# One square per norm: a 1024-column sum of squares in place of two halves, and an epsilon that GpSimd adds

## The chip, the cores and the metric

The program runs on one core of a Trainium2 chip. The metric is the device time of one execution in microseconds (us). Before the change three runs gave 1055.66, 1057.25 and 1059.41 us; the median is 1057.25.

The engines are called by their names in the profile: PE (TensorE, matrix products), ACT (ScalarE), DVE (VectorE), POOL (GpSimd) and SP (SyncE, which issues the transfers). PEld is PE's loading of weights.

## The reference

Two decoder layers on 256 tokens of 1024 columns. Each layer is three half-layers (six in all): a SwiGLU, a mixer (sparse attention in the first layer, differential attention in the second) and a second SwiGLU. Each half-layer has a norm ahead and a norm behind:

```python
def rmsnorm(x, g):
    xf = x.astype(jnp.float32)
    y = xf * lax.rsqrt(jnp.mean(xf * xf, axis=-1, keepdims=True) + EPS)
    return (y * g.astype(jnp.float32)).astype(x.dtype)
...
h = modulate(rmsnorm(x, pre_norm[i, 0]), sh0, sc0)
y = swiglu(h, ffn_w_gate[i, 0], ffn_w_up[i, 0], ffn_w_down[i, 0])
x = x + FFN_HALF * g0[:, None, :] * rmsnorm(y, post_norm[i, 0])
```

The shifts, scales and gates come from a product of a conditioning vector with `ada_w`, in 18 pieces of 1024 columns.

## The kernel before

The 256 tokens are two tiles of 128, `t` = 0 and 1, called t0 and t1 here. The residual stream is in `X[t]`, 128 rows of 1024 columns; two more columns hold a constant whose scaled square is the epsilon. A product is computed for each tile by itself, with weights as the moving operand: a block of 128 rows of a weight matrix is read by SP into `raw`, rounded by ACT (`whl` at line 234, "CAST") and its rest taken by DVE (line 235), because each product is made of three matmuls of rounded parts and rests. So a block of weights is six matmuls for a tile (three kinds, two halves of the columns). There are seven buffers for such blocks (`WBUFS = 7`), and each block is used by t0 and then by t1 before its buffer is free. t1 runs five to seven blocks behind t0 (`LAG`, `LAGX`).

Where one half-layer ends and the next begins, a tile goes through a chain. Its last matmul of `y` (`ydown`, `ydsa` or `ydiff`) ends; `postnorm` takes the sum of squares of `y` on ACT, raises it to the power −0.5 on POOL, and adds to `X[t]` on DVE: first `u`, `y` times the gate, then `x`, `u` times the power plus the old `x`. Then `prenorm` takes the sum of squares of the new `X[t]` on ACT (`normed`), the power on POOL, and DVE makes `h` in two steps (`modulated`): `x` times `g` (line 414), times the power plus `sh` (line 415). PE transposes `h` into `ps_x` (line 418), eight times 128x128, ACT and DVE split that into `HT`, and the next product begins. There are five such places between the six half-layers, and the end of the program is a sixth with `postnorm` alone.

`u` reads `y` in PSUM after ACT's square of it: the framework lets the two engines read that tile in turn. A scheduler sets the order of the instructions on each engine ahead of time, by a model of their durations and by priorities (`urgent()` raises that of the norms); on the chip each engine then keeps to that order. Between the instructions of the chain it places other work, above all casts and subtractions of weights (lines 234 and 235) and the accumulations of `ada_w` on DVE (line 311, `pg`, `g` or `sh`). POOL also clears the buffers of these accumulations (line 302).

The lines that the change touches are `normed` (lines 397 to 408) and `postnorm` (from line 458).

Of the kernel before, what the change touches and what calls it, by code (L numbers as in the profile page):

```python
# [8 lines left out]
F32 = mybir.dt.float32  # L9
F32R = mybir.dt.float32r  # L10
I32 = mybir.dt.int32
AF = mybir.ActivationFunctionType
OP = mybir.AluOpType
# [5 lines left out]
EPS = 1e-6  # L19
# [30 lines left out]
def trunk(ctx, tc, x, c, positions, ada_w, ada_b, pre_norm, post_norm, ffn_w_gate, ffn_w_up,  # L50
          ffn_w_down, dsa_w_in, dsa_w_out, diff_w_in, diff_w_out, diff_lambda, diff_subln, out):
    nc = tc.nc
# [5 lines left out]
    small = ctx.enter_context(tc.tile_pool(name="small", bufs=2))  # L58
# [5 lines left out]
    def tmp(name, shape=(128, 1024), dt=F32):  # L64
        return tmpp.tile(list(shape), dt, name=name, tag="tmp")
# [13 lines left out]
    def half(hf):  # L79
        return slice(hf * 512, (hf + 1) * 512)  # L80

    def flat(t):
        return t.rearrange("p a b -> p (a b)")
# [6 lines left out]
    for t in range(2):  # L90
        xt = consts.tile([128, D + 2], F32, name=f"x{t}")
        nc.vector.memset(xt[:, D:D + 2], EPS_COL)
        X.append(xt)
    epsc = consts.tile([128, 1], F32, name="epsc")
# [302 lines left out]
    def normed(t):  # L397

        xt = X[t]
        ss = small.tile([128, 2], F32, name="ss", tag="ss", bufs=4)  # L400
        r = small.tile([128, 1], F32, name="rstd", tag="rstd1", bufs=4)
        for hf, w in enumerate((512, 513)):
            junk = tmp("junk", (128, 513))
            nc.scalar.activation(junk[:, 0:w], xt[:, hf * 512:hf * 512 + w], AF.Square, scale=1.0 / 32,
                                 accum_out=ss[:, hf:hf + 1])
        nc.scalar.activation(r, ss[:, 0:1], AF.Identity, bias=ss[:, 1:2])
        nc.gpsimd.tensor_tensor(r, r, mhalf[:, 0:1], op=OP.pow)  # L407
        return r, HT[:, t]

# [13 lines left out]
    def first_h(t, k):  # L423

        for q, (f0, n) in enumerate(PIECES):
            if f0 == k * 128 and q not in FIRST:
                FIRST[q] = True
                first_part(q)
                if q == 0:
                    FIRST["x"] = []  # L430
                    for u in range(2):
                        nc.sync.dma_start(X[u][:, 0:D], x[0, u * 128:(u + 1) * 128, :])
                        FIRST["x"].append(normed(u))
                for u in range(2):
                    modulated(0, u, *FIRST["x"][u], k, n // 128)
        return FIRST["x"][t][1]

    def prenorm(t, n):
        r, hT = normed(t)
        for q in range(2):  # L440
            modulated(n, t, r, hT, 4 * q, 4)
        return hT
# [13 lines left out]
                                           op0=OP.mult, op1=OP.subtract)  # L456

    def postnorm(t, y, n, last=False):
        ss = small.tile([128, 2], F32, name="ssy", tag="ssy", bufs=4)
        r = small.tile([128, 1], F32, name="rstdy", tag="rstd1", bufs=4)  # L460
        u = tmp("u")
        for hf in range(2):
            junk = tmp("junk", (128, 513))
            nc.scalar.activation(junk[:, 0:512], y[:, hf, :], AF.Square, scale=1.0 / 32, accum_out=ss[:, hf:hf + 1])
            if hf == 0:
                nc.scalar.activation(ss[:, 0:1], ss[:, 0:1], AF.Identity, bias=epsc)
        nc.scalar.activation(r, ss[:, 0:1], AF.Identity, bias=ss[:, 1:2])  # L467
        nc.gpsimd.tensor_tensor(r, r, mhalf[:, 0:1], op=OP.pow)  # L468
        for hf in range(2):
            nc.vector.tensor_tensor(u[:, half(hf)], y[:, hf, :], MOD[n]["pg"][:, half(hf)], op=OP.mult)  # L470
        for hf in range(2):
            h = half(hf)
            nc.vector.scalar_tensor_tensor(X[t][:, h], u[:, h], r, X[t][:, h], op0=OP.mult, op1=OP.add)
            if last:
                nc.sync.dma_start(out[0, t * 128:(t + 1) * 128, h], X[t][:, h])
# [9 lines left out]
    def ffn(t, n):  # L485
# [86 lines left out]
        with urgent():  # L572
            postnorm(t, y, n, last=(n == 5))
# [50 lines left out]
    def dsa(t, n):  # L624
# [151 lines left out]
        with urgent():  # L776
            postnorm(t, y, n)

    def diff(t, n):
# [134 lines left out]
        with urgent():  # L914
            postnorm(t, y, n)
# [73 lines left out]
```

## Time and profile before

| | |
|---|---|
| median of three runs | 1057.25 us |
| the profiled execution | 1058.01 us |
| its span, first to last instruction | 1056.2 us |
| PE busy | 1015.5 us, 96% |
| DVE busy | 788.6 us, 75% |
| ACT busy | 523.8 us, 50% |
| POOL busy | 45.0 us, 4% |
| mean granted clock of PE | 0.993 |

In a timeline a row gives the start in us, the duration in us, the engine, the line of the kernel, the operation and what it writes and reads; the brackets hold the idle time ahead of it and what ended that. In a row of waits come the engine and what it waited for, then the total in us, the number of times and the longest. In a row of windows the stretch is followed by its length, the busy time of PE, PEld, DVE, ACT and POOL with their instructions, the granted clock of PE, the busy share of the transfer engines and GB/s. In a group there are the total busy us and the mean ns of one.

### The profile page before, as it was taken

The numbers are of one execution on the slowest core, as the hardware profiler recorded it, in microseconds if no ns is written. First come the engines' busy times: TensorE is split into PE (matmuls) and PEld (weight loads), VectorE is DVE, ScalarE is ACT, GpSimd is POOL, SyncE is SP. The second block draws the span as 40 slices with busy tenths as digits, with TensorE's granted clock in tenths as the row PEclk, the third lists the DMA queues.
The fourth block names the chain that finished last, engine by engine and source line by source line (L and its number), as shares of the span: only waits on it lengthen the run. The fifth ranks groups of instructions, "written<-read, shape, count | busy, mean of one in ns | idle before, by whom it ended". The sixth has DMA issues, their size and how long they took to land.

```text
span 1056.2 us, 15311 instructions
## 1 busy us (share of the span) xinstructions
PE 1015.5 (96%) x5936; PEld 873.6 (83%) x5936; DVE 788.6 (75%) x1121; ACT 523.8 (50%) x834; POOL 45.0 (4%) x49
## 2 busy tenths in 40 slices
PE   5999999989999999999999999999999899999997
PEld 2689997769778789998878999887777678999875
DVE  5769887989976977877688967767988575765643
ACT  3354534455575654543455544346477555544432
POOL 1000000001000200000030000001000120000000
PEclk9999999999999999999999999999999999999999
DMA  9959899986443477988757979956653443778431
GB/s 315 343 147 322 313 321 378 347 293 218 148 142 128 155 273 247 352 286 291 271 193 260 314 257 316 316 208 236 260 200 118 153 134 115 243 235 261 183 117 40
DMA packets 93732, 249.48 MB, mean 236 GB/s; under 512 B 6084, under 2 KB 24652, under 8 KB 93660
## 3 DMA queue, kind: packets, MB, share of 16 engines
q1 hardware_dynamic: 93660, 248.52, 68.1%
q8 instruction: 46, 0.75, 0.3%
q14 instruction: 26, 0.21, 0.1%
HBM read 247.44 MB, written 1.05 MB: 235 GB/s over the span
## 4 chain that ended last, share of the span: by engine, by line
PE 57%; issue 20%; DVE 4%; ACT 3%; POOL 2%; DMA 1%; POOLq 0%; DVEq 0%; ACTq 0%
PE ydown L267 15%; PE up L282 9%; PE gate L282 8%; PE gate L267 3%; PE up L267 3%; PE projQd L267 2%; PE projQ L267 2%; PE projV L267 2%; PE projA L267 2%; PE projK L267 2%; PE ydsa L267 1%; POOL rstd L407 1%; DVE whl L235 1%; PE dsaO L752 1%; PE ydiff L267 1%
## 5 line engine op out<-in xcount | busy, mean ns | idle before, releaser
L235 DVE TENSOR_TENSOR whl<-raw,whl 128x1024 fp32r<-128x1024 f32 (+3 forms) x216 | 245.7, 1150 | 98.5 <-ACT whl L234 97.7
L234 ACT CAST whl<-raw 128x1024 fp32r<-128x1024 f32 (+3 forms) x216 | 211.8, 995 | 190.1 <-PE ydown L267 89.5
L282 PE MATMUL gate<-HT,wj 128*128 128x256 f32 x1344 | 166.2, 284 | 1.5 <-DVE wj L212 1.4
L212 DVE TENSOR_TENSOR wj<-raw,wj 128x1024 fp32r<-128x1024 f32 x112 | 134.7, 1221 | 43.1 <-ACT wj L211 42.8
L211 ACT CAST wj<-raw 128x1024 fp32r<-128x1024 f32 x112 | 116.4, 1050 | 100.3 <-DMA raw<-in_ffn_w_up_dram 21.5
L282 PEld LDWEIGHTS gate<-HT,wj 128*128 128x128 f32 x1344 | 163.4, 192 | 2.2 <-DVE wj L212 1.9
L282 PE MATMUL up<-HT,wj 128*128 128x256 f32 x1344 | 164.4, 283 | 0.0
L282 PEld LDWEIGHTS up<-HT,wj 128*128 128x128 f32 x1344 | 162.8, 192 | 0.4
L267 PE MATMUL ydown<-whl,ffj 128*128 128x512 f32 x672 | 157.0, 390 | 2.2 <-DVE whl L235 2.2
L267 PEld LDWEIGHTS ydown<-whl,ffj 128*128 128x128 f32 x672 | 125.7, 188 | 30.6 <-DVE whl L235 3.1
L267 PE MATMUL gate<-whl,HT 128*128 128x480 f32 x384 | 94.3, 392 | 0.4 <-ACT HT L393 0.2
L267 PE MATMUL ydown<-whl,ffa 128*128 128x512 f32 (+1 forms) x368 | 89.3, 393 | 1.9 <-ACT whl L234 1.9
L267 PEld LDWEIGHTS gate<-whl,HT 128*128 128x128 f32 x384 | 72.2, 191 | 16.6 <-ACT HT L393 2.7
L267 PEld LDWEIGHTS ydown<-whl,ffa 128*128 128x128 f32 (+1 forms) x368 | 67.9, 188 | 19.7 <-issue 3.6
L311 DVE SCALAR_TENSOR_TENSOR pg<-araw,scond,pg 128x1024 f32<-128x1024 f32 x48 | 61.4, 1280 | 6.4 <-DMA araw<-in_ada_w_dram 5.8
L267 PE MATMUL up<-whl,HT 128*128 128x480 f32 x288 | 66.0, 381 | 0.0
L267 PEld LDWEIGHTS up<-whl,HT 128*128 128x128 f32 x288 | 53.5, 188 | 8.4 <-ACT sg L512 0.5
L311 DVE SCALAR_TENSOR_TENSOR g<-araw,scond,g 128x1024 f32<-128x1024 f32 x40 | 51.2, 1281 | 7.8 <-DMA araw<-in_ada_w_dram 7.4
L311 DVE SCALAR_TENSOR_TENSOR sh<-araw,scond,sh 128x1024 f32<-128x1024 f32 x40 | 51.2, 1280 | 1.3 <-DMA araw<-in_ada_w_dram 0.8
L468 POOL TENSOR_TENSOR rstdy<-rstdy,mhalf 128x1 f32<-128x1 f32 x12 | 10.2, 850 | 824.2 <-ACT rstdy L467 824.2
L267 PE MATMUL projV<-whl,HT 128*128 128x512 f32 x96 | 28.4, 416 | 0.0
L267 PE MATMUL projQ<-whl,HT 128*128 128x512 f32 x96 | 27.6, 415 | 0.0
(224 smaller groups left out, 1090.7 us busy)
## 6 DMA issues: line engine op xcount, KB each, us to landing
araw<-in_ada_w_dram SPq DMA_DIRECT2D x64, 1024.0 KB
raw<-in_ffn_w_down_dram SPq DMA_DIRECT2D x40, 1024.0 KB
raw<-in_ffn_w_gate_dram SPq DMA_DIRECT2D x56, 512.0 KB
raw<-in_ffn_w_up_dram SPq DMA_DIRECT2D x56, 512.0 KB
raw<-in_ffn_w_gate_dram SPq DMA_DIRECT2D x16, 960.0 KB
raw<-in_diff_w_in_dram SPq DMA_DIRECT2D x12, 1024.0 KB
raw<-in_ffn_w_up_dram SPq DMA_DIRECT2D x12, 960.0 KB
fraw<-in_ada_w_dram SPq DMA_DIRECT2D x32, 256.0 KB
```

Of the source, the lines that this page charges most:

```text
L211: nc.scalar.copy(hl[0], raw)
L212: nc.vector.tensor_tensor(hl[1], raw, hl[0].bitcast(F32), op=OP.subtract)
L234: nc.scalar.copy(hl[:, 0, 0:n], raw[:, j, 0:n])
L235: nc.vector.tensor_tensor(hl[0:r, 1, 0:n], raw[0:r, j, 0:n], hl[0:r, 0, 0:n].bitcast(F32), op=OP.subtract)
L267: nc.tensor.matmul(acc[:, hf, 0:n], lhs, rhs, start=(first and hf not in seen), stop=(last and i % 3 == 2))
L282: nc.tensor.matmul(a[:, b, :], w[:, wp, j, b * 128:(b + 1) * 128], HT[:, :, hp, k0 + j, :], start=(first and j == 0 and i == 0 and b % 2 = ...
L311: nc.vector.scalar_tensor_tensor(a, raw[:, j, :], scond[:, 2 * i + j:2 * i + j + 1], a, op0=OP.mult, op1=OP.add)
L407: nc.gpsimd.tensor_tensor(r, r, mhalf[:, 0:1], op=OP.pow)
L468: nc.gpsimd.tensor_tensor(r, r, mhalf[:, 0:1], op=OP.pow)
L752: nc.tensor.matmul(flat(O)[:, h * 64:(h + 1) * 64], ptb[u][:, i * nb + b, :], v[:, b, :], start=(b == 0), stop=(b == nb - 1), skip_group_c ...
```

## The change

Each sum of squares becomes one ACT operation over all columns, which writes its sum straight to `r`. In the pre-norm it goes over 1025 columns, the constant among them. In the post-norm the epsilon was the bias of an ACT addition and is now added by POOL, ahead of its power.

```diff
     def normed(t):
         xt = X[t]
-        ss = small.tile([128, 2], F32, name="ss", tag="ss", bufs=4)
         r = small.tile([128, 1], F32, name="rstd", tag="rstd1", bufs=4)
-        for hf, w in enumerate((512, 513)):
-            junk = tmp("junk", (128, 513))
-            nc.scalar.activation(junk[:, 0:w], xt[:, hf * 512:hf * 512 + w], AF.Square, scale=1.0 / 32,
-                                 accum_out=ss[:, hf:hf + 1])
-        nc.scalar.activation(r, ss[:, 0:1], AF.Identity, bias=ss[:, 1:2])
+        junk = tmp("junk", (128, 1025))
+        nc.scalar.activation(junk, xt[:, 0:1025], AF.Square, scale=1.0 / 32, accum_out=r)
         nc.gpsimd.tensor_tensor(r, r, mhalf[:, 0:1], op=OP.pow)
         return r, HT[:, t]
...
     def postnorm(t, y, n, last=False):
-        ss = small.tile([128, 2], F32, name="ssy", tag="ssy", bufs=4)
         r = small.tile([128, 1], F32, name="rstdy", tag="rstd1", bufs=4)
         u = tmp("u")
-        for hf in range(2):
-            junk = tmp("junk", (128, 513))
-            nc.scalar.activation(junk[:, 0:512], y[:, hf, :], AF.Square, scale=1.0 / 32, accum_out=ss[:, hf:hf + 1])
-            if hf == 0:
-                nc.scalar.activation(ss[:, 0:1], ss[:, 0:1], AF.Identity, bias=epsc)
-        nc.scalar.activation(r, ss[:, 0:1], AF.Identity, bias=ss[:, 1:2])
+        junk = tmp("junk")
+        nc.scalar.activation(junk, flat(y), AF.Square, scale=1.0 / 32, accum_out=r)
+        nc.gpsimd.tensor_scalar(r, r, EPS, None, op0=OP.add)
         nc.gpsimd.tensor_tensor(r, r, mhalf[:, 0:1], op=OP.pow)
```

The scheduler makes another order of it. The lines of the changed kernel are numbered 4 to 8 lower from here on: 414 became 410, 418 is 414, 464 is 458, 470 is 462, 473 is 465.

PE, at the third place, from the second SwiGLU of the first layer to the first of the second. Before (`ydown` in the first rows is t1's; t0's last `ydown` stands 41 matmuls ahead of the first transposes; `gate` is t0's; the eight `ps_x` at the end are t1's):

```order
L418 MATMUL ps_x<-ident,h 128x128 x4
L267 MATMUL ydown<-whl,ffj 128x512
L418 MATMUL ps_x<-ident,h 128x128 x4
L267 MATMUL gate<-whl,HT 128x480 x38
L418 MATMUL ps_x<-ident,h 128x128 x8
```

With the change (t0's last `ydown` stands 35 matmuls ahead of the first transposes):

```order
L414 MATMUL ps_x<-ident,h 128x128 x4
L267 MATMUL ydown<-whl,ffj 128x512
L414 MATMUL ps_x<-ident,h 128x128 x4
L267 MATMUL gate<-whl,HT 128x480 x4
L267 MATMUL ydown<-whl,ffj 128x512 x2
L267 MATMUL gate<-whl,HT 128x480 x20
L267 MATMUL ydown<-whl,ffj 128x512 x4
L267 MATMUL gate<-whl,HT 128x480 x18
L414 MATMUL ps_x<-ident,h 128x128 x8
```

Six matmuls of t1's `ydown` moved from ahead of t0's transposes to between those of t0's `gate`; t1's last `ydown` now has 18 matmuls between it and t1's transposes. The second, fourth and fifth place have the same pattern, with 31 matmuls ahead of t0's first transposes at each; at the first place PE's order is as before.

ACT, at the fifth place, from the differential attention to the last SwiGLU, t0's chain. Before:

```order
L464 ACTIVATE junk,ssy<-ydiff 128x512 x2
L466 ACTIVATE ssy<-ssy,epsc 128x1
L234 CAST whl<-raw 128x960
L467 ACTIVATE rstdy<-ssy 128x1
L234 CAST whl<-raw 128x960 x2
L404 ACTIVATE junk,ss<-x_79 128x512
L404 ACTIVATE junk,ss<-x_79 128x513
L234 CAST whl<-raw 128x960
L406 ACTIVATE rstd<-ss 128x1
```

With the change:

```order
L458 ACTIVATE junk,rstdy<-ydiff 128x1024
L234 CAST whl<-raw 128x960 x2
L402 ACTIVATE junk,rstd<-x_79 128x1025
L234 CAST whl<-raw 128x960 x3
L393 CAST HT<-ps_x 128x512 x2
```

No cast stands any more between the square and the sum that POOL takes.

DVE, at the same place, t0's chain. Before:

```order
L470 TENSOR_TENSOR u<-ydiff,pg 128x512 x2
L235 TENSOR_TENSOR whl<-raw,whl 128x960
L473 SCALAR_TENSOR_TENSOR x_79<-u,rstdy,x_79 128x512 x2
L235 TENSOR_TENSOR whl<-raw,whl 128x960
L414 TENSOR_TENSOR h<-x_79,g 128x512 x2
L235 TENSOR_TENSOR whl<-raw,whl 128x960
L415 SCALAR_TENSOR_TENSOR h<-h,rstd,sh 128x512 x2
```

With the change:

```order
L462 TENSOR_TENSOR u<-ydiff,pg 128x512 x2
L465 SCALAR_TENSOR_TENSOR x_79<-u,rstdy,x_79 128x512 x2
L235 TENSOR_TENSOR whl<-raw,whl 128x960
L410 TENSOR_TENSOR h<-x_79,g 128x512 x2
L411 SCALAR_TENSOR_TENSOR h<-h,rstd,sh 128x512 x2
```

Two of the three weight subtractions left the chain; the one between `x` and `h` stayed. At the third place an accumulation of line 311 now stands ahead of t0's `u`.

## The prediction

> **What bounds the kernel now.** I read the busy rows of the page first, then the waits of PE, then PE's timeline at the five places where one half-layer ends and the next begins, then ScalarE, VectorE and GpSimd there.
>
> ```profile
> PE 1015.5 (96%) x5936; PEld 873.6 (83%) x5936; DVE 788.6 (75%) x1121; ACT 523.8 (50%) x834; POOL 45.0 (4%) x49
> ...
> PE ps_x L418 <- DVE h L415: 10.7, 9, 3.4
> ```
>
> TensorE works 96% of the span. Nothing that shortens ScalarE (50%) or loads GpSimd (4%) counts by itself; what counts is how long PE stands still. Its largest wait is the transposes `ps_x` of a new half-layer waiting for `h`: 10.7 us. Here are these places, called b1 to b5. Token tile 0 (t0) is transposed first, tile 1 (t1) some 30 matmuls later.
>
> ```profile
> 236.22 1.77 PE L418 MATMUL ps_x<-ident,h 128*128 128x128 f32 x8 [3.39 <-DVE h L415]
> ...
> 347.67 1.38 PE L418 MATMUL ps_x<-ident,h 128*128 128x128 f32 x8 [1.36 <-DVE h L415]
> 349.00 8.76 PE L267 MATMUL gate<-whl,HT 128*128 128x480 f32 x32
> 357.60 1.03 PE L418 MATMUL ps_x<-ident,h 128*128 128x128 f32 x8
> ...
> 523.76 16.03 PE L267 MATMUL ydown<-whl,ffj 128*128 128x512 f32 x70
> 540.64 0.66 PE L418 MATMUL ps_x<-ident,h 128*128 128x128 f32 x4 [0.85 <-DVE h L415]
> 541.97 8.59 PE L267 MATMUL gate<-whl,HT 128*128 128x480 f32 x38
> 550.71 1.29 PE L418 MATMUL ps_x<-ident,h 128*128 128x128 f32 x8 [0.16 <-DVE h L415]
> ...
> 732.03 1.32 PE L418 MATMUL ps_x<-ident,h 128*128 128x128 f32 x8 [0.82 <-DVE h L415]
> 741.00 0.65 PE L418 MATMUL ps_x<-ident,h 128*128 128x128 f32 x4 [0.36 <-DVE h L415]
> 742.33 0.50 PE L267 MATMUL projK<-whl,HT 128*128 128x512 f32 x1 [0.68 <-ACT HT L393]
> ...
> 860.76 0.63 PE L418 MATMUL ps_x<-ident,h 128*128 128x128 f32 x4 [1.02 <-DVE h L415]
> 862.07 8.57 PE L267 MATMUL gate<-whl,HT 128*128 128x480 f32 x38
> 870.74 1.29 PE L418 MATMUL ps_x<-ident,h 128*128 128x128 f32 x8
> ```
>
> The brackets are PE's idle time. t0 costs 3.39, 1.36, 0.85, 0.82 and 1.02 us; t1 costs next to nothing, since 26 to 38 matmuls of t0's next product lie ahead of its transposes. A matmul takes 16.03/70 = 0.229 us with 512 columns and 8.59/38 = 0.226 us with 480. t0's last `y` matmul (E0) ends where its first square starts:
>
> ```profile
> 228.56 0.60 ACT L464 ACTIVATE junk<-ydown 128x512 f32<-128x512 f32 x1 [5.48 <-PE ydown L267]
> 338.63 0.60 ACT L464 ACTIVATE junk<-ydsa 128x512 f32<-128x512 f32 x1 [0.73 <-PE ydsa L267]
> 721.73 0.60 ACT L464 ACTIVATE junk<-ydown 128x512 f32<-128x512 f32 x1 [3.02 <-PE ydown L267]
> 850.55 0.60 ACT L464 ACTIVATE junk<-ydiff 128x512 f32<-128x512 f32 x1 [3.09 <-PE ydiff L267]
> ```
>
> From E0 to t0's transposes at b5 are 860.76 − 850.55 = 10.2 us. What fills them, ScalarE, GpSimd and VectorE in turn (the last four rows are t1's):
>
> ```profile
> 851.89 0.99 ACT L234 CAST whl<-raw 128x960 fp32r<-128x960 f32 x1
> 852.78 0.30 ACT L467 ACTIVATE rstdy<-ssy 128x1 f32<-128x1 f32 x1
> ...
> 853.15 1.46 POOL L468 TENSOR_TENSOR rstdy<-rstdy,mhalf 128x1 f32<-128x1 f32 x1 [9.68 <-ACT rstdy L467]
> 857.99 1.84 POOL L407 TENSOR_TENSOR rstd<-rstd,mhalf 128x1 f32<-128x1 f32 x1 [3.38 <-ACT rstd L406]
> ...
> 851.85 1.29 DVE L470 TENSOR_TENSOR u<-ydiff,pg 128x512 f32<-128x512 f32 x2 [3.13 <-ACT junk L464]
> 853.05 1.15 DVE L235 TENSOR_TENSOR whl<-raw,whl 128x960 fp32r<-128x960 f32 x1
> 854.65 1.42 DVE L473 SCALAR_TENSOR_TENSOR x<-u,rstdy,x 128x512 f32<-128x512 f32 x2 [0.45 <-POOL rstdy L468]
> 855.98 1.15 DVE L235 TENSOR_TENSOR whl<-raw,whl 128x960 fp32r<-128x960 f32 x1
> 857.05 1.29 DVE L414 TENSOR_TENSOR h<-x,g 128x512 f32<-128x512 f32 x2
> 858.26 1.15 DVE L235 TENSOR_TENSOR whl<-raw,whl 128x960 fp32r<-128x960 f32 x1
> ...
> 865.00 0.55 POOL L468 TENSOR_TENSOR rstdy<-rstdy,mhalf 128x1 f32<-128x1 f32 x1 [5.17 <-ACT rstdy L467]
> 868.36 1.45 POOL L407 TENSOR_TENSOR rstd<-rstd,mhalf 128x1 f32<-128x1 f32 x1 [2.80 <-ACT rstd L406]
> ...
> 864.53 1.28 DVE L470 TENSOR_TENSOR u<-ydiff,pg 128x512 f32<-128x512 f32 x2
> 868.12 1.29 DVE L414 TENSOR_TENSOR h<-x,g 128x512 f32<-128x512 f32 x2
> 869.85 1.41 DVE L415 SCALAR_TENSOR_TENSOR h<-h,rstd,sh 128x512 f32<-128x512 f32 x2 [0.44 <-POOL rstd L407]
> ```
>
> Two things are to be seen. A weight cast of 0.99 us stands between the two additions on ScalarE, so the sum reaches GpSimd only at 853.1. And GpSimd's one-column power takes 0.55 us beside `u`, which reads PSUM (865.00), but with a subtraction or product from SBUF on VectorE it ends about 0.4 us after that: 868.36 + 1.45 = 869.81 against 868.12 + 1.29 = 869.41; 853.15 + 1.46 = 854.61 against 853.05 + 1.15 = 854.20.
>
> **The change, part by part.** *Removed from ScalarE:* per norm one square with its accumulator read and one or two additions, 24 norms. ScalarE is idle half the time, so this pays only through the chain. *The single square:* two halves take 851.85 − 850.55 = 1.28 us with the reads; one pass over 1024 columns of PSUM is bounded below by the activation of that shape:
>
> ```profile
> L558 ACT ACTIVATE sgj<-gate 128x1024 f32<-128x1024 f32 x12 | 12.3, 1026 | 20.0 <-PE gate L282 20.0
> ```
>
> I take 1.13 us, 1.03 and the tail of one read (bounds 1.03 and 1.28). It can no longer start on half the columns, which costs nothing behind `y` (both halves follow E0 already). In the pre-norm it waits for both halves of `x`, but the power behind it waits for VectorE's product `h` anyway. *GpSimd's new addition, 12 times:* no such operation is in the trace; the bounds are the power alone (0.55) and at its most held up (1.84). I take 0.55, since it falls beside `u`, as the row at 865.00 does: addition and power end 1.2 us after the square, `u` 1.3 us. So VectorE's `u` gates `x`, and the addition is hidden; without that cover it costs up to 1.2 us per norm.
>
> *The chain from the last `y` matmul to the transposes* becomes: square 1.15, `u` 1.31, `x` to the next VectorE instruction 1.33 (854.65 to 855.98), a weight subtraction 1.07 (to 857.05), product and power up to the start of `h` 1.73 (868.12 to 869.85), `h` to the transpose 0.89 (869.85 to 870.74): 7.5 us for either tile. t0 had 10.2; 2.7 us are gained.
>
> *What the scheduler makes of it* decides. At b2 to b5 t0's transposes now stand behind 31, 35, 31 and 31 matmuls of t1's `y` (34, 41, 42, 41 before). The rest of that `y` is threaded into t0's next product, and its last matmul (E1) stands behind 24 matmuls of that product. Behind E1 only 18 remain ahead of t1's transposes, where 26 to 38 and t0's transposes stood before. 24 + 18 = 42 are seven weight blocks of six: all seven buffers are then full, and t0 can't run on. 18 matmuls are 4.1 us and t1's chain is 7.5, so PE stands still for 3.4 us four times. Work on b5: t0's transposes at 850.55 + 7.5 = 858.05 (PE gets there at 850.55 + 31·0.229 = 857.65, a stall of 0.4 for 1.02); transposes with the matmul between them 1.3 us (860.76 to 862.07); 24·0.226 + 10·0.229 = 7.7; E1 = 867.05; t1's transposes at 874.55. By then 42 matmuls of the product are done, before 38: less 4·0.226 this is 873.65 against 870.74, a loss of 2.9.
>
> In the same way: b2 346.15 + 1.3 + 5.9 + 7.5 = 360.8, less 10 matmuls 2.3, against 357.60: +0.9. At b3 E0 is 540.64 − 0.85 − 41·0.229 = 530.4, and a modulation accumulation has moved ahead of `u`, whose data were requested late:
>
> ```profile
> L311 DVE SCALAR_TENSOR_TENSOR g<-araw,scond,g 128x1024 f32<-128x1024 f32 x40 | 51.2, 1281 | 7.8 <-DMA araw<-in_ada_w_dram 7.4
> ```
>
> It costs 0 to 1.5 us, I take 0.8: 538.7 + 1.3 + 6.8 + 7.5 = 554.3, less 0.9, against 550.71: +2.7. b4: 729.2 + 1.3 + 38·0.229 + 7.5 = 746.7, less 16·0.229 = 3.7, against 741.00 and the 0.68 behind it: +1.3. At b1 the order of PE stays and t0's chain loses the additions: −0.5. The end of the program is gated by `u` before and after: 0. Other rows that changed places (transfers, a weight subtraction here and there) are costed at nothing, hidden behind PE. Sum: −0.5 + 0.9 + 2.7 + 1.3 + 2.9 = +7.3 us.
>
> *The clock.* A stall has an echo:
>
> ```profile
> 346.09:349.50 3.41, 1.95 (x11) 1.31 (x11) 2.97 (x5) 2.95 (x7) 0.73 (x1) 1.00 0.09 37
> 349.50:352.91 3.41, 3.41 (x10) 2.80 (x10) 3.41 (x6) 1.93 (x5) 1.50 (x2) 0.50 0.74 222
> ```
>
> These are windows of 3.41 us; PE was busy 1.95 us of the first, mostly transposes, and was granted half the clock (0.50) in the next. 32 matmuls took 357.60 − 349.00 = 8.6 us there instead of 7.2: a loss of 1.4. The new stalls are longer, but whether a window holds enough of one depends on its phase. I take two of four: +2.8. (The loss at b2 is already left out of its sum.) The Trainium skill, in "TensorE: Matmul & The Clock Gate", Part 1, has the half clock follow a whole idle window of about 3.4 us; by that rule no new stall would trigger it and the sum would be 7.3. Its Part 4 says that transposes don't count as activity; the row at 346.09 goes with that, and with less than a whole idle window.
>
> Total +10.1 against the profiled execution, 1058.01 (span 1056.2 and 1.8 around it), which lies 0.8 above the median 1057.25: 1067.4.
>
> **Rivals.** *No slow windows (1064.6):* the stalls come, split by the seventh weight block, and no window holds enough idleness. For it: b5's stall of 1.02 had no echo. Against: the row at 346.09. *Heavier (1078):* GpSimd's addition is held up as the power at 857.99, 1.2 us on each of eight chains, and all the stalls grow. Against: 865.00. *Faster (1053):* t1's chain is covered after all. Then the t0 stalls fall by 2.5 us, b1 by 0.5, the slow window at b2 by 1.4. It decides where the chain from E1 is under 4.1 us; against it, `u` and `x` alone are 2.7 and the square 1.1. *No difference (1060):* the delay is given back because the stretch after a boundary is paced by VectorE, which uses the stall to prepare weights:
>
> ```profile
> 552.00:570.00 18.00, 17.99 (x82) 15.24 (x83) 17.49 (x17) 9.62 (x10) 0.24 (x1) 1.00 0.70 230
> ```
>
> For it: VectorE is busy 17.49 of 18 us there. Against: PE is busy 17.99, 0.219 us a matmul, so it doesn't wait for it.
>
> **How the numbers follow.** Forecast 0.48, no slow windows 0.18, heavier 0.12: slower 0.78. No difference 0.13, faster 0.09. About 0.3% (3.2 us) is what a measurement of this kernel tells from no change, so slower begins at 1060.4. The forecast's own range is 1063 to 1073, an error of 1 us per boundary and none to four slow windows. The range given reaches down to 1057, half of the no-difference case, and up to 1077, short of the heaviest: it leaves out 0.09, 0.06 and 0.05.
>
> **What would show it.** In the changed kernel's PE timeline `ps_x` of t0 at b2 to b5 waits about 0.4 us and `ps_x` of t1 about 1.5, with a second wait of about as much for the weights just ahead of it; the waits of PE on `h` grow from 10.7 to some 13 us, and new ones on `whl` come in. GpSimd's addition reads about 0.55 us. Granted clocks of 0.50 stand behind two of the t1 stalls. The prediction is wrong if t1's transposes wait under 1 us, if the addition takes over 1.3, or if the stretches behind the boundaries are shorter than before.

## The result, and the profile after

The changed kernel took 1070.32 us (median of four runs, 1065.92 to 1073.45) against 1056.51 for the kernel before on the same chip: 1.0118 times as long, 95% interval 1.0089 to 1.0148. Run again beside other kernels it took 1067.36 (six runs, 1064.81 to 1073.53), 1.0094 times, interval 1.0066 to 1.0121. (A ratio here is estimated from all runs of both kernels, so it can differ in the third decimal from the quotient of the medians.) The profiled execution took 1068.36 us, its span 1066.6. The page's busy row and the rows of PE's waits after:

```profile
PE 1020.6 (96%) x5936; PEld 876.7 (82%) x5936; DVE 790.6 (74%) x1121; ACT 511.4 (48%) x750; POOL 41.4 (4%) x61
...
PE ps_x L414 <- DVE h L411: 9.4, 9, 2.8
PE gate L267 <- DVE whl L235: 5.8, 3, 2.0
...
PE projK L267 <- DVE whl L235: 1.9, 1, 1.9
```

ACT lost 12.4 us of work (511.4 for 523.8), and the kernel is slower all the same. The wait for `h` is not longer (9.4 for 10.7), but two rows are new, those on `whl`: PE waits four times, 7.7 us in all, for the rest of a block of weights. PE's timeline shows where, here at b2, b3 and b5 (line 414 was 418 before):

```profile
347.87 0.66 PE L414 MATMUL ps_x<-ident,h 128*128 128x128 f32 x4 [0.35 <-DVE h L411]
...
360.12 1.13 PE L267 MATMUL gate<-whl,HT 128*128 128x480 f32 x4 [1.95 <-DVE whl L235]
362.08 1.75 PE L414 MATMUL ps_x<-ident,h 128*128 128x128 f32 x8 [0.83 <-DVE h L411]
...
549.89 1.09 PE L267 MATMUL ydown<-whl,ffj 128*128 128x512 f32 x4
550.82 3.20 PE L267 MATMUL gate<-whl,HT 128*128 128x480 f32 x14
555.95 1.17 PE L267 MATMUL gate<-whl,HT 128*128 128x480 f32 x4 [1.94 <-DVE whl L235]
557.91 1.94 PE L414 MATMUL ps_x<-ident,h 128*128 128x128 f32 x8 [0.79 <-DVE h L411]
...
864.98 0.63 PE L414 MATMUL ps_x<-ident,h 128*128 128x128 f32 x4
...
878.89 1.13 PE L267 MATMUL gate<-whl,HT 128*128 128x480 f32 x4 [1.94 <-DVE whl L235]
880.85 1.75 PE L414 MATMUL ps_x<-ident,h 128*128 128x128 f32 x8 [0.83 <-DVE h L411]
```

t0's transposes wait 0.35 us at b2, 0.57 at b3 and nothing at b4 and b5, where they waited 0.8 to 1.4. t1's, which waited for next to nothing, stand behind 2.73 to 2.78 us of idle time at these three places and 2.56 at b4, the two waits taken together. At b3 `y` of t1 ends at 551.07, 14 + 4 matmuls of t0's product follow, and the transposes come at 557.91, 6.84 us later. The wait for weights belongs to the same chain. The rest of the seventh block stands on VectorE behind t1's `x`, as its timeline and those of ScalarE and GpSimd show:

```profile
551.07 1.03 ACT L458 ACTIVATE junk<-ydown 128x1024 f32<-128x1024 f32 x1 [5.60 <-PE ydown L267]
...
552.22 1.29 DVE L462 TENSOR_TENSOR u<-ydown,pg 128x512 f32<-128x512 f32 x2 [1.07 <-ACT junk L458]
553.43 1.41 DVE L465 SCALAR_TENSOR_TENSOR x<-u,rstdy,x 128x512 f32<-128x512 f32 x2
554.75 1.15 DVE L235 TENSOR_TENSOR whl<-raw,whl 128x960 fp32r<-128x960 f32 x1
555.82 1.28 DVE L410 TENSOR_TENSOR h<-x,g 128x512 f32<-128x512 f32 x2
557.02 1.41 DVE L411 SCALAR_TENSOR_TENSOR h<-h,rstd,sh 128x512 f32<-128x512 f32 x2
...
552.27 0.22 POOL L459 TENSOR_SCALAR rstdy<-rstdy 128x1 f32<-128x1 f32 x1 [10.30 <-ACT junk L458]
552.58 0.57 POOL L460 TENSOR_TENSOR rstdy<-rstdy,mhalf 128x1 f32<-128x1 f32 x1
...
556.15 0.76 POOL L403 TENSOR_TENSOR rstd<-rstd,mhalf 128x1 f32<-128x1 f32 x1 [1.63 <-ACT junk L402]
```

GpSimd's addition and power are over at 553.15, ahead of `x` at 553.43, which had to wait for `u`. The echo on the clock is there too, one window of 3.41 us later, at b2, b3 (two windows) and b5, but not at b4:

```profile
17.59:21.00 3.41, 1.65 (x7) 0.48 (x5) 2.62 (x6) 1.68 (x4) 2.64 (x3) 1.00 1.09 359
21.00:24.41 3.41, 3.41 (x9) 2.85 (x10) 3.25 (x6) 2.21 (x4) 0.00 (x0) 0.50 1.10 366
358.92:362.33 3.41, 1.38 (x7) 0.95 (x8) 3.41 (x6) 1.15 (x2) 1.71 (x2) 1.00 0.03 10
362.33:365.75 3.42, 3.42 (x13) 2.74 (x12) 3.33 (x5) 1.17 (x2) 0.95 (x1) 0.50 0.01 2
553.48:556.89 3.41, 1.47 (x7) 0.80 (x5) 3.41 (x6) 1.15 (x2) 1.69 (x2) 1.00 1.00 403
556.89:560.30 3.41, 2.62 (x11) 2.13 (x11) 3.38 (x5) 1.00 (x2) 1.92 (x3) 0.50 0.07 24
560.30:563.72 3.42, 3.42 (x10) 2.87 (x9) 2.09 (x4) 1.17 (x2) 0.00 (x0) 0.50 0.10 16
...
751.45:754.87 3.42, 1.95 (x9) 1.19 (x10) 3.42 (x6) 0.91 (x3) 1.77 (x2) 1.00 0.01 4
754.87:758.28 3.41, 3.40 (x15) 2.42 (x16) 3.41 (x4) 2.04 (x3) 0.00 (x0) 1.00 0.00 1
```

The first two rows are at the very start, where the kernel before had no such window; the last two are b4.

### The profile page after: what moved, and what is told of

Read it like the earlier page. It is cut to its first block, busy times and chain, and to the rows that moved or that the text cites. A ratio compares the mean times of both kernels' runs of the same rounds, so it can differ in the third digit from the quotient of the medians.

```text
span 1066.6 us, 15260 instructions
## 1 busy us (share of the span) xinstructions
PE 1020.6 (96%) x5936; PEld 876.7 (82%) x5936; DVE 790.6 (74%) x1121; ACT 511.4 (48%) x750; POOL 41.4 (4%) x61
## 4 chain that ended last, share of the span: by engine, by line
PE 81%; DVE 8%; DMA 5%; ACT 3%; issue 2%; POOL 1%; SPq 0%; DVEq 0%; ACTq 0%; POOLq 0%
PE ydown L267 22%; PE up L282 13%; PE gate L282 12%; PE gate L267 6%; PE up L267 5%; PE projQd L267 2%; PE projQ L267 2%; DMA fraw<-in_ada_w_dram 2%; PE ydsa L267 2%; PE projK L267 2%; PE projV L267 2%; PE projA L267 2%; DVE whl L235 2%; PE ydiff L267 1%; DVE wj L212 1%
## 5 line engine op out<-in xcount | busy, mean ns | idle before, releaser
L267 PE MATMUL gate<-whl,HT 128*128 128x480 f32 x384 | 99.5, 403 | 5.9 <-DVE whl L235 5.8
L267 PEld LDWEIGHTS gate<-whl,HT 128*128 128x128 f32 x384 | 75.2, 199 | 23.1 <-DVE whl L235 7.0
L311 DVE SCALAR_TENSOR_TENSOR pg<-araw,scond,pg 128x1024 f32<-128x1024 f32 x48 | 61.4, 1280 | 10.7 <-DMA araw<-in_ada_w_dram 10.3
L459 POOL TENSOR_SCALAR rstdy<-rstdy 128x1 f32<-128x1 f32 x12 | 3.8, 315 | 841.5 <-ACT junk L458 841.5
```

The costliest lines, as they stand in the source:

```text
L267: nc.tensor.matmul(acc[:, hf, 0:n], lhs, rhs, start=(first and hf not in seen), stop=(last and i % 3 == 2))
L311: nc.vector.scalar_tensor_tensor(a, raw[:, j, :], scond[:, 2 * i + j:2 * i + j + 1], a, op0=OP.mult, op1=OP.add)
L459: nc.gpsimd.tensor_scalar(r, r, EPS, None, op0=OP.add)
```

## The experiments

Theory A is the prediction's: the loss is the order on PE. Presumably because t0's chain got shorter, the scheduler lets t0's next product begin before t1's `y` has ended; t1's chain then starts late, with too few matmuls ahead of its transposes. Theory B: the operations themselves cost it, GpSimd's addition and the square that can't start on a half. Theory C: windows of half clock come as they like, whatever the order. Each kernel ran beside the kernel before on one chip, and ratios are to that. Where windows of half clock are counted, the stretch at half clock with which every trace ends is left out.

**The order alone.** The arithmetic stays; the last two steps of t1's `y` get a higher priority (the same edit stands in `matmuls` for `ydsa` and `ydiff`):

```diff
+YPRI = 300
+YTAIL = 2
...
+    def early(on):
+        return tc.high_priority(offset=YPRI) if on else nullcontext()
...
         for k, (a, rows) in enumerate(acts):
             yield
-            mm(t, y, a, 0, (512, 512), k == 0, k == len(acts) - 1, rows=rows)
+            with early(t and k >= len(acts) - YTAIL):
+                mm(t, y, a, 0, (512, 512), k == 0, k == len(acts) - 1, rows=rows)
```

> The changed kernel, with the last two steps of token tile 1's `y` (12 matmuls at most) given a higher priority: on TensorE they then end before tile 0's next product begins, and 26 to 32 matmuls of that product stand between them and tile 1's transposes (18 in the changed kernel). The arithmetic is that of the changed kernel. Theory A (the loss is the order on TensorE: the chain of 6.8 us behind tile 1's last `y` matmul stands behind 18 matmuls of 0.229 = 4.1 us): 32 matmuls are 7.3 us, so the waits at b2 to b5 for weights and for tile 1's `h` (1.95 + 0.83, 1.94 + 0.79, 1.89 + 0.67, 1.94 + 0.83 = 10.8 us) go, and with them the windows of half clock behind them (four of about 1.5 us): 1070.3 - 10.8 - 6 = 1053.5, between 1051 and 1057. Theory B (the operations themselves cost it: GpSimd's addition, the square that can't start on a half): the order changes nothing of them, 1066 to 1070. Theory C (the half-clock windows come as they like, at the start and elsewhere, whatever the order): only the waits go, 1059 to 1060.

> The changed kernel with the last two steps of tile 1's `y` ahead once more, beside the other orders on one chip and for a second trace (the profiled execution of the first stood 10 us above the median of its runs, with eight windows of half clock in the attention parts). Theory A: 1051 to 1055, no wait for weights ahead of tile 1's transposes. Theory C: the windows in the attention parts stand elsewhere or in another number than in the first trace, and the span less 1.6 us for each is again about 1048.

Measured: 1052.59 us (twelve runs, 1049.92 to 1063.0), 0.9963 of the kernel before, interval 0.9942 to 0.9984; and again 1052.54 (1050.44 to 1056.47), 0.9959, interval 0.9939 to 0.9978. PE's timeline of the second, at b3:

```profile
535.56 2.56 PE L272 MATMUL ydown<-whl,ffj 128*128 128x512 f32 x10
537.96 7.10 PE L272 MATMUL gate<-whl,HT 128*128 128x480 f32 x32
545.62 1.29 PE L419 MATMUL ps_x<-ident,h 128*128 128x128 f32 x8 [0.56 <-DVE h L416]
```

The ten last matmuls of `y` now precede the product, 32 of its matmuls stand behind them, and the wait for weights is gone. The same additions and squares that cost 9.8 to 13.8 us in one order save 3.6 to 4.8 in another: theory B falls, and this version beats both kernels. It isn't only that it has fewer windows of half clock: of the runs with a mean granted clock of 0.997, four with `y` ahead took 1050.44 to 1051.99 us, and thirteen of the kernel before on the same chip 1054.36 to 1056.43. The first trace's eight windows of half clock all lie at the start, in the stretch up to b1's product and in the attention, none behind t1's transposes at b2 to b5. The second trace has one window, and its span is 11.5 us shorter (1049.7 for 1061.2), 1.6 us for each of the seven.

**Half the dose.** The same with `YTAIL = 1`:

> The changed kernel with only the last step of tile 1's `y` given the higher priority (the run with the last two steps gave 1052.6). At b2 all of `y` then ends ahead of tile 0's product with 32 matmuls behind it, at b3 to b5 it ends behind 18 matmuls of that product and has 24 behind it (18 in the changed kernel). It is the dose between the two. Theory A: 24 matmuls cover 5.5 of the chain's 6.85 us, so PE waits 1.2 to 1.5 us ahead of tile 1's transposes at b3, b4 and b5 (2.6 to 2.8 in the changed kernel) and not at b2: 1067.4 to 1070.3 less 2.8 + 3 x 1.35 = 6.9, less one to three windows of half clock of 1.5 us: 1057 to 1062. Theory B: 1066 to 1070.

Measured: 1059.41 us (twelve runs, 1055.73 to 1061.95), 1.0016, interval 0.9998 to 1.0034: between the two, as A says. The waits are less even than expected: PE's idle time ahead of t1's transposes is 2.78 us at b3, 1.21 at b4 and 2.01 at b5, where 1.2 to 1.5 was said. At b3 the 24 matmuls gained nothing, since VectorE's accumulation of `g` came just ahead of `u`, so that the chain took 551.04 − 542.89 = 8.15 us:

```profile
543.63 1.28 DVE L316 SCALAR_TENSOR_TENSOR g<-araw,scond,g 128x1024 f32<-128x1024 f32 x1
544.83 1.28 DVE L467 TENSOR_TENSOR u<-ydown,pg 128x512 f32<-128x512 f32 x2
...
544.09 0.90 POOL L464 TENSOR_SCALAR rstdy<-rstdy 128x1 f32<-128x1 f32 x1 [10.01 <-ACT junk L463]
```

The chain at b4 is 6.81 and at b5 7.37 us.

**The addition, taken away and doubled.** Two kernels whose order on PE is that of the changed one:

```diff
-        nc.gpsimd.tensor_scalar(r, r, EPS, None, op0=OP.add)
```

> The changed kernel without GpSimd's addition of epsilon behind a product: that part of the computation is left out. TensorE's order is the same as in the changed kernel at all five places. It prices the addition (0.22 us in the rows of the changed kernel, 12 times). Theory A: it lies beside VectorE's `u` and is hidden, 1069 to 1071.5, with the waits for weights and `h` at b2 to b5 as they were. Theory B: the addition lengthens every chain by 0.3 to 1.2 us, eight chains and the end: 1060 to 1068.

```diff
-        nc.gpsimd.tensor_scalar(r, r, EPS, None, op0=OP.add)
+        nc.gpsimd.tensor_scalar(r, r, EPS / 2, None, op0=OP.add)
+        nc.gpsimd.tensor_scalar(r, r, EPS / 2, None, op0=OP.add)
```

> The changed kernel with GpSimd's addition of epsilon in two halves, one behind the other, so twice the additions; TensorE's order is that of the changed kernel. With the run without the addition it prices it from the other side. Theory A (hidden beside VectorE's `u`): one more addition of 0.22 us brings 0.2 us at most per chain, 1069 to 1072. Theory B (a GpSimd operation of one column is held up by VectorE's instructions, 0.55 to 1.2 us each on eight chains): 1074 to 1080.

Measured: without it 1068.4 us (six runs), 1.0115, interval 1.0093 to 1.0137; doubled 1067.3 (four runs), 1.0079, interval 1.0055 to 1.0103. Both lie where the changed kernel does (1.0094 and 1.0118). The times alone don't tell the theories apart here: 1068.4 is just below the 1069 of theory A and just above the 1068 of theory B, and 1067.3 is below both ranges of its expectation. The chains do. The chain from t1's last `y` matmul to its transposes, at b2 to b5: 6.85, 6.84, 6.82, 6.84 us in the changed kernel; 6.90, 6.90, 6.87, 6.90 with two additions; 7.37, 6.85, 7.35, 6.84 with none. So one more addition costs 0.06 us of a chain, and without the one in the change no chain is shorter: it is hidden.

**One norm of the two.**

```diff
# the norm behind a product as in the change, the norm ahead of it as before
-        junk = tmp("junk", (128, 1025))
-        nc.scalar.activation(junk, xt[:, 0:1025], AF.Square, scale=1.0 / 32, accum_out=r)
+        for hf, w in enumerate((512, 513)):
+            ...
+        nc.scalar.activation(r, ss[:, 0:1], AF.Identity, bias=ss[:, 1:2])
```

and the other way round:

> Only the norm behind a product is changed (single square, GpSimd's addition); the norm ahead of a product is as before (two squares and an addition). In the order that results tile 1's last `y` matmul stands behind 4 matmuls of tile 0's next product at b3 to b5, and 25 to 34 stand between it and tile 1's transposes; at b2 all of `y` comes first, with 32 behind it. Theory A: no place has the late `y`, 25 to 34 matmuls are 5.7 to 7.8 us against a chain of 6.8 to 7.8, so at most about 1 us is lost anywhere and tile 0's chain is shorter: 1053 to 1058. Theory B: all twelve additions and all twelve squares of the costly kind are in, 1065 to 1070. Theory C: anything from 1053 to 1065, by the number of half-clock windows in its trace.

> Only the norm ahead of a product is changed (one square over 1025 columns); the norm behind a product is as before, so there is no addition on GpSimd. In the order that results only b4 has the late `y` (18 matmuls of tile 0's product ahead of the last ones and 18 behind); at b3 and b5 34 matmuls stand behind tile 1's last `y`, at b2 32. Theory A: one place with a wait of 2.5 to 3 us and perhaps a window of half clock of 1.5 behind it, the rest as before or up to 1 us better: 1056 to 1061, and its trace has a wait for weights ahead of tile 1's transposes at b4 alone. Theory B: without the addition as before or faster, 1053 to 1056.

Measured: the norm behind alone 1053.38 us (twelve runs, 1049.9 to 1058.73), 0.9966, interval 0.9943 to 0.999. All twelve additions are in, and it is faster: again against B. The norm ahead alone 1065.55 (five runs, 1065.19 to 1067.17), 1.0092, interval 1.0078 to 1.0106, which neither theory gave. Its one late place is b4, as A says, but PE stands idle there for 3.91 us where 2.5 to 3 was said:

```profile
742.77 3.43 PE L267 MATMUL projK<-whl,HT 128*128 128x512 f32 x14
746.80 1.19 PE L267 MATMUL projK<-whl,HT 128*128 128x512 f32 x4 [0.60 <-DVE whl L235]
751.31 1.40 PE L414 MATMUL ps_x<-ident,h 128*128 128x128 f32 x8 [3.31 <-DVE h L411]
```

With its echo that is 4.4 us from t0's last `y` at b4 to that at b5 (858.14 − 724.91 against 850.55 − 721.73). Another 4.3 us are lost before b2 (342.96 against 338.63), in the attention, where three windows in a row, from 322.34 to 332.58, are at half clock while PE's row shows it busy:

```profile
317.12:320.53 3.41, 3.41 (x23) 2.34 (x21) 1.31 (x6) 2.61 (x9) 0.00 (x0) 1.00 0.03 12
...
322.30:325.70 3.40, 3.40 (x15) 2.52 (x14) 1.15 (x5) 0.60 (x2) 0.00 (x0) 0.51 0.00 0
325.70:329.20 3.50, 3.50 (x15) 2.98 (x14) 2.36 (x7) 1.77 (x6) 0.00 (x0) 0.50 0.02 5
```

All five runs of this version have a low mean granted clock (0.985 to 0.989), so the windows seem to come in each. They are not its own, though: the second trace of the changed kernel, below, has three at the same place, and its first has none. What brings them stays open.

**An eighth weight buffer.** The control has the second edit alone:

```diff
-WBUFS = 7
+WBUFS = 8
-BIGBUFS = 11
+BIGBUFS = 9
```

> The changed kernel with eight weight buffers in place of seven (and nine activation buffers in place of eleven, to make room). At b3, b4 and b5 24 + 24 = 48 matmuls of tile 0's product (eight blocks of six) stand ahead of tile 1's transposes in place of 24 + 18 = 42; `y` of tile 1 ends behind the same 24 as before, and it now does so at b2 too. Theory A (the seventh weight buffer limits how far tile 0 runs ahead under tile 1's chain of 6.8 us): 24 matmuls cover 5.5 us in place of 4.1, so PE's wait ahead of tile 1's transposes falls from 2.6-2.8 us to 1.2-1.4 at b3, b4, b5. Against its control with seven weight and nine activation buffers it is then 4 us faster at b3 to b5 and 1.3 slower at b2, with fewer half-clock windows. Theory B (the operations) or a chain that is limited elsewhere: the wait stays at 2.6 us and above.

> The control for eight weight buffers: the changed kernel with nine activation buffers in place of eleven and seven weight buffers as they were. At b3, b4 and b5 the order on TensorE is that of the changed kernel (tile 1's last `y` matmul behind 24 matmuls of tile 0's product, 18 behind it); at b2 all of `y` now comes ahead of the product, with 32 matmuls behind it. Theory A: the waits at b3 to b5 are as in the changed kernel (2.6 to 2.8 us each), the one of 2.8 at b2 is gone, with its half-clock window: 1065 to 1068 if nine activation buffers cost nothing else. Theory B: 1069 to 1071, the waits unrelated to the order.

Measured: 1075.74 us (six runs, 1070.28 to 1082.12), 1.0164, interval 1.0123 to 1.0204; the control 1075.57 (1070.08 to 1085.12), 1.0188, interval 1.015 to 1.0227. The whole time tells nothing between them, and the control's 1065 to 1068 was missed. The nine activation buffers are the only edit of the control, so the cost is theirs; where it arises was not looked into. The waits do tell. At b3, control first, then eight buffers:

```profile
546.45 3.20 PE L267 MATMUL gate<-whl,HT 128*128 128x480 f32 x14
551.59 1.13 PE L267 MATMUL gate<-whl,HT 128*128 128x480 f32 x4 [1.94 <-DVE whl L235]
553.55 1.29 PE L414 MATMUL ps_x<-ident,h 128*128 128x128 f32 x8 [0.83 <-DVE h L411]
```

```profile
562.61 4.28 PE L267 MATMUL gate<-whl,HT 128*128 128x480 f32 x19
567.75 1.36 PE L267 MATMUL gate<-whl,HT 128*128 128x480 f32 x5 [0.86 <-DVE whl L235]
569.71 1.29 PE L414 MATMUL ps_x<-ident,h 128*128 128x128 f32 x8 [0.60 <-DVE h L411]
```

24 matmuls for 18, and 1.46 us of idle time for 2.77: six more matmuls cover 1.31 us, about what they take (6 · 0.226 = 1.36). At b4 the idle time is 1.21 for 1.89, and at b5 2.00 for 2.77, with a chain of 7.36 us. The seventh buffer is the limit.

**The changed kernel once more.**

> The changed kernel once more, for its spread and a second trace. Both theories: 1066 to 1073, with the waits at b2 to b5 within 0.3 us of those of the first trace, since they follow from the order. Theory C (half-clock windows fall by their phase, which is free): the windows at half clock stand at other places or in another number; the one near 21 us, which cost 2.4 us at the start, is there only when the windows begin at about the same time modulo 3.41 us as in the first trace.

Its times stand with the result above. The waits ahead of t1's transposes are the same to 0.05 us (chains 6.84, 6.84, 6.81, 6.84). The windows of half clock aren't: none at the start, where t0's first `y` ends at 228.57 (before 228.56, in the first trace 231.01), but three in the attention (322 to 333 us), two each at b2 and b4, one each at b3 and b5. Its rows at the start:

```profile
17.50:21.00 3.50, 1.93 (x9) 1.27 (x10) 3.47 (x8) 2.69 (x5) 2.38 (x3) 1.00 1.10 357
21.00:24.40 3.40, 3.40 (x13) 1.92 (x12) 3.20 (x6) 1.20 (x3) 0.00 (x0) 1.00 1.10 371
```

Here the grid of windows starts at 2.02 us modulo 3.41, in the first trace at 0.52. The version with `y` ahead shows the same pair: a half-clock window at 21 us in its first trace (grid at 0.9) and none in its second (grid at 2.6). All fourteen traces of this case bear it out: the six whose grid stands between 3.36 and 0.92, past the turn at 3.41, have the window at the start, and the eight between 1.34 and 3.06, the kernel before among them, haven't.

**Two more orders.** The norm behind alone with `y` ahead, and the changed kernel with `YTAIL = 4` and `YPRI = 600`:

> Only the norm behind a product is changed, and the last two steps of tile 1's `y` are given the higher priority: a candidate that may beat both kernels. At b3 to b5 `y` then ends ahead of tile 0's product in place of behind 4 of its matmuls. Theory A: nothing waited there before, so no difference to the version without the priority beyond the spread: 1051 to 1055, 0.996 to 0.998 of the kernel before.

> The changed kernel with the last four steps of tile 1's `y` given a priority above that of tile 0's norm: at b2 to b5 tile 0's transposes stand behind all of tile 1's `y` again (32 to 42 matmuls, as in the kernel before), and 23 to 34 matmuls of tile 0's product stand between them and tile 1's transposes. Theory A: tile 0's chain of 6.85 us lies behind 9.6 us of `y` at b3 to b5 and no tile waits there; at b1, where the order of the two `y` is turned round, it is as before: 1050 to 1054. Theory B: 1066 to 1070.

Measured: 1056.46 us (twelve runs, 1049.8 to 1060.74), 0.9987, interval 0.9964 to 1.0011: no gain over the versions above, and outside the 1051 to 1055 that were expected. Its runs go with the granted clock: three at 0.999 took 1049.80 to 1051.51, four at 0.989 took 1059.66 to 1060.74. The trace is one of the latter and has six windows of half clock, four of them in the attention. And 1059.42 (twelve runs, 1056.46 to 1061.52), 1.0013, interval 0.9999 to 1.0028, where 1050 to 1054 were expected: b2 to b5 have no wait for `h` at t0 and at most 0.39 us at t1, with 0.87 to 0.89 for weights at each place, but the loss moved to b1, where the turned order leaves t0's chain uncovered, which the expectation had passed over:

```profile
232.67 2.20 PE L272 MATMUL ydown<-whl,ffj 128*128 128x512 f32 x9
241.93 1.97 PE L419 MATMUL ps_x<-ident,h 128*128 128x128 f32 x8 [7.06 <-DVE h L416]
```

**What is the wait and what the clock.** From t0's last `y` matmul at b3 to that of the last half-layer, three places lie in one stretch. A window of half clock cost 1.4 us in the prediction's working; its number is counted in each trace:

| kernel | stretch, us | PE idle in it, us | half-clock windows | stretch less 1.4 for each |
|---|---|---|---|---|
| before | 509.1 | 8.3 | 1 | 507.7 |
| changed, first and second trace | 515.7, 517.1 | 12.9, 13.0 | 3, 4 | 511.5, 511.5 |
| two additions; none | 517.1; 514.9 | 13.2; 13.2 | 4; 2 | 511.5; 512.1 |
| half the dose | 511.1 | 10.3 | 1 | 509.7 |
| `y` ahead, first and second trace | 504.1, 505.5 | 6.2, 6.3 | 0, 1 | 504.1, 504.1 |
| norm behind alone | 504.6 | 6.1 | 0 | 504.6 |
| norm behind alone, `y` ahead | 505.4 | 7.0 | 0 | 505.4 |
| norm ahead alone | 513.3 | 11.2 | 2 | 510.5 |
| four steps of `y` ahead | 506.4 | 6.8 | 1 | 505.0 |

These rows bound the stretch before and, the last two, after; the row between is the one window of half clock in it before, in the mixer behind b4:

```profile
530.53 0.60 ACT L464 ACTIVATE junk<-ydown 128x512 f32<-128x512 f32 x1 [3.02 <-PE ydown L267]
1039.59 0.60 ACT L464 ACTIVATE junk<-ydown 128x512 f32<-128x512 f32 x1 [3.02 <-PE ydown L267]
...
830.78:834.20 3.42, 3.42 (x19) 3.42 (x18) 2.59 (x3) 0.63 (x1) 0.00 (x0) 0.50 0.28 109
...
534.41 1.03 ACT L458 ACTIVATE junk<-ydown 128x1024 f32<-128x1024 f32 x1 [3.08 <-PE ydown L267]
1050.12 1.03 ACT L458 ACTIVATE junk<-ydown 128x1024 f32<-128x1024 f32 x1 [3.08 <-PE ydown L267]
```

The two traces of one kernel agree to 0.1 us once the windows are taken off (without the addition it is 0.6 more, and b4's chain 0.5 longer). PE's idle time needs no price for a window, and it puts the kernels in the order that theory A says. Of the loss in this stretch, 6.6 and 8.0 us in the two traces, 4.6 and 4.7 are idle time; in the rest, 2.0 and 3.3, PE is busy for longer, with two and three more windows of half clock. A window can lie partly over the idle time, as the one at 556.89 does, and then costs less than 1.4. Theory C has this much truth, that where and how often the echo comes differs between executions. The other part of C falls: with `y` ahead the windows behind t1's transposes are gone with the waits.

## Why the prediction was right, and where it wasn't

The time (1067.4 for 1070.3 and 1067.4), the direction and the mechanism held: t1's late chain, behind the 18 matmuls that the buffers allow, is what costs the time. That the sum came so near is luck: for the profiled execution it said 10.1 us and 10.4 were measured, but the places were put too high by 3.5, the echoes too low by 2.8, and 1.0 came from two stretches that were not in the sum, the start and the mixer behind b4. Its steps, by the first trace against that of before:

- *The order and the seven blocks.* Shown by the runs with `y` ahead and with eight buffers: 18 matmuls stood ahead of t1's transposes, and t0 could not run on. Why the scheduler chose that order was not tested.
- *The chain, 7.5 us.* Mis-sized: 6.84 at t1, and 864.98 − 858.14 = 6.84 at t0 of b5. The term that failed is "product and power up to the start of `h` 1.73": it took 557.02 − 555.82 = 1.20. The power (0.76 us) ended 0.4 us behind the first of VectorE's two products, at 556.91, instead of 0.4 behind the second, which ended at 557.10. `u` gave the rest, 1.21 for 1.31. So the idle time is 2.6 to 2.8 per place, not 3.4.
- *The sum of the places.* Between t0's last `y` matmuls the spans grew by −0.5 (b1), 1.9 (b2), 4.7 (b3), −1.0 (b4) and 2.9 us (b5). Taking off 1.4 for each echo of the changed kernel, and 1.4 from the kernel before at b4 for a window in the mixer, leaves −0.5, 0.5, 1.9, 0.4 and 1.5, where −0.5, 0.9, 2.7, 1.3 and 2.9 were said: 3.8 for 7.3. The shorter chain makes 2.6 of the difference (0.66 at four places), t0's remaining wait at b5, put at 0.4 and gone, another 0.4; 0.5 stays unassigned. With the four echoes at 5.6, the mixer's window at −1.4 and the start at 2.4 this adds up to 10.4, as the spans differ (1066.6 − 1056.2). The busy rows give another split, without a price for windows: PE stood idle for 46.0 us (span less busy time) where it was 40.7, and was busy for 1020.6 where it was 1015.5.
- *The late accumulation at b3, 0.8 us.* It was there: VectorE waited 2.90 us for its data ahead of t0's `u`, and t0's chain took 542.81 − 534.41 = 8.40 us, 1.56 more than at b5; 8.3 was said, with the chain put too long and this term too short. t0's transposes waited 0.57.
- *Two of four echoes, 2.8 us.* Four windows behind three places, 5.6; six behind four places in the second trace. At b4 of the first trace a window with 1.95 us of PE work had no echo, and at b2 of the kernel before one with 1.95 had: busy time alone doesn't decide it. The Trainium skill, in "TensorE: Matmul & The Clock Gate", Part 1, wants a whole idle window ahead of the half clock, and the rows at 358.92 and 553.48 (1.38 and 1.47 us of work, then 0.50) speak against that, as the one at 346.09 did.
- *The start, nothing.* It cost 2.4 us in the first trace, with a half-clock window at 21 us; the second trace of the same kernel has neither, and over all traces the window goes with the phase of the grid: it is not the change. The mixer's window, which of the two traces only that of before had, gave 1.4 back. Neither was in the sum.
- *The addition, 0.55 us beside `u`.* It took 0.22 at ten of twelve places, and it is hidden, as said. At t0 of b3 it took 1.24, beside the late accumulation, which held up `u` as well. The single square, 1.13, took 1.15 up to the start of `u` (552.22 − 551.07).
- *The rivals.* "Heavier" needed additions held up by 1.2 us on eight chains; it happened on one, and a second addition costs 0.06. "Faster" (1053) is what the version with `y` ahead took, where the order covers t1's chain. "No difference" did not come: PE's idle time grew by 5.3 us over the span. "No slow windows" didn't either: four and six stand behind t1's transposes in the two traces.
- *The signs.* The new waits on `whl` came, but the idle time was divided otherwise than said: 1.9 us on weights and 0.7 to 0.8 on `h` instead of 1.5 each, and the waits on `h` fell to 9.4 in all instead of growing to 13. By the letter, then, a sign of being wrong came true, since t1's transposes wait under 1 us; what it was to show, a chain that is covered after all, did not, for the wait for weights just ahead is the same chain's. The stretch behind b4 is 1.0 us shorter than before, by the mixer's window that the changed kernel didn't have.

## What to carry to other kernels

When a scheduler places the instructions, an edit that shortens one chain can move the start of another: compare the order on the bound engine at the places that wait before pricing any operation. Where two tiles share buffers, the tile that leads can hide the other's chain only as far as the buffers let it run, so the end of the trailing tile's product should come before the leading tile's next one begins. And an idle time of 2 to 3 us on PE can cost half as much again in the clock window behind it (1.4 us in this kernel), so times of single runs are compared with the number of such windows beside them.

## What the runs showed of the hardware that was not expected

- The grid of 3.41 us windows stood at another phase in each traced execution (0.52 and 2.02 us modulo 3.41 in the changed kernel, 0.9 and 2.6 with `y` ahead), and the windows of half clock differ with the execution: the changed kernel's two traces have 6 and 10 of them and spans of 1066.6 and 1071.7 us. The Trainium skill, in "TensorE: Matmul & The Clock Gate", Part 1, calls the window free-running, and the pairs of traces agree.
- Half clock also came in the attention while PE's rows show 3.4 us of 3.4 busy, with transposes and short matmuls (the rows at 322.30 and 325.70 above). The same stretch ran at full clock in the first trace of the changed kernel, where PE was as busy.
- A one-column power on GpSimd that starts 0.34 us into VectorE's first product can end 0.4 us behind the first (0.76 us, at 360.32 in the changed kernel, with the product from 359.98) or behind the second (1.36 us, at 360.11 without the addition, with the product from 359.76). Between the two it steps by one VectorE instruction, and what decides the step was not settled.
